# A decoder trunk's MLP: the norm's factor 1/rms² moved from the up projection to the token-major output, and the up weights regrouped

## The chip, the cores and the metric

The kernel runs on one core of one Trainium2 chip. The metric is the device time of one execution in microseconds, the median of several runs; beside it there is one profiled execution, whose trace the text reads. The engines are TensorE (PE: matmuls; PEld: its weight loads), VectorE (DVE), ScalarE (ACT), GpSimd (POOL) and SyncE (SP, which issues most of the DMAs).

## What is computed

A trunk of two layers over 512 tokens of width 1024, all in float32. Layer 0 mixes tokens with a gated DeltaNet, layer 1 with a convolution module; each layer then has a cross-attention into a memory of 256 tokens, and an MLP. The change is in the MLP:

```
def rms_norm(x, g):
    return x * rsqrt(mean(x * x, axis=-1) + 1e-6) * g

def sq_relu_mlp(h, w_up, w_down):        # w_up (1024, 4096), w_down (4096, 1024)
    return square(relu(h @ w_up)) @ w_down

h = h + sq_relu_mlp(rms_norm(h, mlp_norm[layer]), w_up[layer], w_down[layer])
```

After the second layer a final rms_norm is applied. The factor 1/rms is one positive number per token. So relu commutes with it, the square makes it 1/rms², and it may be multiplied in before the relu, or once per token behind the down projection.

## The kernel before

**Precision.** A float32 product is made of three matmuls in a rounded format: each operand is split into a high part (a cast, on ScalarE) and a low part (the operand minus its high part, on VectorE), and `mm3` (line 290) issues high x high, low x high and high x low into one PSUM bank. TensorE's 7298 matmuls are mostly of this kind.

**Weights.** All weights come through one list of units of 128 x 1024 values (`order`, `loads`, `need`; lines 150 to 220). `wload` (line 227) issues a unit's DMA from SP into a `raw` buffer, of which there are six; units of the down projection that are sums of weight blocks get DMAs with accumulation from GpSimd's queue (`more`, line 237). `wsplit` (line 241) casts a unit into `wh` on ScalarE (line 251) and subtracts on VectorE into `wl` (line 255, recorded under the helper's line 71). `wnext` (line 264) hands out the next unit and first issues the loads and splits of units ahead: three `wh`/`wl` pairs exist (`NW`), so the split of a unit can start when the unit three before it has been used.

**The MLP** (`mlp7`, line 1078) goes over the 4096 hidden columns in four groups of 1024 (`g`). In each group there is first the up projection, then the down projection.

- Up: hidden columns are rows of the result, tokens its columns. Eight tiles of 128 x 512 are made, each from one weight unit of 1024 rows by 128 columns with 24 matmuls of 512 columns (`proj`). `up_ev` (line 1096) takes a bank out: VectorE does max(., 0) x `rb` (`rl`), ScalarE squares it (`u`). `rb` holds 1/rms of every token, spread over all partitions. It is made in `Norm.stat` (line 401): two matmuls with a matrix of ones (`ssq`), a Sqrt on ScalarE, a reciprocal on VectorE (`rb`, line 408). They are issued inside the second up unit of group 0, and the first bank is taken out only after that (the list `first`). Tiles come in pairs (hidden blocks 0 and 4, 1 and 5, ...); `early` (line 1106) prepares the first of a pair for the down projection and `late` (line 1110) both: sums, differences and splits of 256-column halves.
- Down: the product is made by a scheme that needs seven block products for eight (`dn7`, line 1121). Tokens are rows. Each product takes two weight units and fills two banks, which `evict` and `into` (lines 1151 and 1160) add into accumulators `acc` on VectorE, or copy there on ScalarE if the accumulator is new. In the last group an order of its own applies (`LAST7`), in which the product T2 is followed by six accumulations from SBUF to SBUF.
- Residual: in layer 0 the accumulators are transposed back at the end (`outs`). In layer 1 the residual is transposed into the accumulators during group 0 (`turn`, line 1088), and after the last group `final` (line 1208) applies the last norm: squares with a sum on ScalarE, a Sqrt, a reciprocal on VectorE, two scalings, and the output DMA.
- In layer 0, group 3, `mid` calls `mem_gain` (line 885) between up and down: 16 operations on the memory for the next layer, half on ScalarE and half on VectorE.

**Order.** The program is written as one sequence. The framework makes the semaphores and gives each engine one fixed sequence, close to the order of the text; an engine doesn't overtake in its own sequence at run time. Buffers of 128 x 512 come from one pool of 69 (`slot`).

Of the kernel before, what the change touches and what calls it, by code (L numbers as in the profile page):

```python
# [10 lines left out]
AF = mybir.ActivationFunctionType  # L11
# [26 lines left out]
def tile_trunk(ctx, tc, xT, memT, x_d, mem_d, prm_d, adt_d, bdw_d, tap_d, fin_d, w_ab, w_kq, w_v, w_z, w_dno, w_pw1, w_pw2,  # L38
# [144 lines left out]

    def plan_mlp7(layer):
        for g in range(4):
            for i in range(4):
                plan(("up", layer, g * 4 + i), w_up[layer, g * 4 + i])
# [53 lines left out]
    def wsplit():  # L241
# [5 lines left out]
        raw = combos7(i, j[0], hf) if kind == "dn7" else ws["raw"].pop(need[u])  # L247
# [13 lines left out]
        if kind == "dn7":  # L261
            after7(i, j[0], hf)

    def wnext(key, hf):
        i = ws["next"]
        assert order[i] == (key, hf), (order[i], key, hf)
        while ws["load"] <= need[min(i + NRAW + 1 + 2 * (order[i][0][0] in ("up", "dn7")), len(order) - 1)]:
            wload()
# [3 lines left out]
        return ws["hl"].pop(i)  # L272

# [94 lines left out]
    class Norm:  # L368
        def __init__(self, gname):
            self.g, self.acc, self.xs, self.n, self.side = gname, None, [], 0, None  # L370
# [12 lines left out]
        def square(self, h, e=pool, side=False):  # L383
# [12 lines left out]
            if self.n == KT:  # L396
                if self.side:
                    tt(dve, self.acc, self.acc, self.side, ALU.add)
                self.hl = split(self.acc, "sq")
# [678 lines left out]
    def mlp7(layer, norm, hres, nxt=None, mid=None):  # L1078
# [9 lines left out]
        def turn(i):  # L1088
# [4 lines left out]
            act.copy(a, ps)  # L1093
            acc[n, m, c] = a

        def up_ev(ps):
            t = slot(s="rl")
            stt(t, ps, 0.0, norm.rb, ALU.max, ALU.mult)
            u = slot(s="u2")
            act.activation(u, t, AF.Square)  # L1100
            return u
# [19 lines left out]
        def dn7(g, ops):  # L1121
# [29 lines left out]
            def into(key, c, ps, op=ALU.add):  # L1151
                k = key + (c,)
                if k not in acc:
                    acc[k] = acc_tile(key)
                    act.activation(acc[k], ps, AF.Copy, scale=1.0 if op == ALU.add else -1.0)
                else:
# [531 lines left out]
    n2 = Norm("mlp_norm0")  # L1688
# [5 lines left out]
    n5 = Norm("mlp_norm1")  # L1694
# [13 lines left out]
ACC_CV = (("p",), (1, 0), (0, 0))  # L1708
ORDER7 = [("11", "11", "a", True), ("R3", "T3", "b", True), ("S1", "T1", "c", True), ("12", "21", "a", False),
# [78 lines left out]
def _layout(np, i):  # L1788
# [36 lines left out]
    halves = [8 * g + m for g in range(4) for m in (0, 4, 1, 5, 2, 6, 3, 7)]  # L1825
    r["w_up"] = np.stack([_pack_a(np, i["mlp_w_up"][j], halves) for j in range(2)])
# [19 lines left out]
```

## Time and profile before

| | |
|---|---|
| median of 3 runs | 1466.11 us (1464.77 to 1466.46) |
| the profiled execution's own time | 1465.14 us |
| its span in the trace | 1463.4 us |
| granted TensorE clock, mean | 0.998 |
| busy: TensorE, VectorE, ScalarE, GpSimd | 99%, 73%, 53%, 18% |
| MLP of layer 0, first up matmul | at 473.4 us |
| MLP of layer 1, last up stage ends, last operation | about 1418 us, 1459 us |

The trace gives each instruction's start and duration, and for a wait what ended it. Lines are line numbers of the kernel; where a helper records an operation the line is the helper's (71 for `tt`, 77 for `stt`), so one goes by the tile's name: `wl<-raw,wh` is an operation that reads `raw` and `wh` and writes `wl`. A TensorE matmul's duration contains its way through the array; the distance between two starts is its pace.

### The profile page before, as it was taken

Reading aid. Unit: us, or ns where it says so; the run is one execution under the profiler, and the core shown is the slowest. Engines: PE = TensorE matmul, PEld = TensorE weight load, DVE = VectorE, ACT = ScalarE, POOL = GpSimd, SP = SyncE. Lnnn points to the kernel's source line nnn. Section 1 sums busy time; section 2 is a strip of 40 time slices with the busy share of each in tenths; the row PEclk is TensorE's granted clock in tenths of the full one; section 3 lists DMA queues with packets and bytes.
Section 4 is the critical chain, followed back from the end, with each engine's and each line's share of the span. In section 5 each row is a group of like instructions: output and inputs, shape, how many; then the busy total and the mean of one; then the engine's idle time right before and its main releaser. Section 6 shows DMA issues by size and latency. Waiting matters only on the chain.

```text
span 1463.4 us, 19623 instructions
## 1 busy us (share of the span) xinstructions
PE 1452.9 (99%) x7298; PEld 1225.5 (84%) x7298; DVE 1065.2 (73%) x1615; ACT 771.2 (53%) x1326; POOL 266.8 (18%) x289
## 2 busy tenths in 40 slices
PE   9999999999999999999999999999999999999997
PEld 7888889988888888888888889988888888888886
DVE  6879889867646766767679899985555776767677
ACT  7766865655434464435355655564444544434354
POOL 1411310103113000010000486402113010000100
PEclk9999999999999999999999999999999999999999
DMA  8232124442213666584766624533214566575853
GB/s 283 84 115 73 59 87 158 132 143 87 72 44 108 166 165 179 140 199 136 202 159 215 185 82 162 179 129 100 72 51 127 139 169 177 135 210 131 229 144 87
DMA packets 62735, 201.82 MB, mean 138 GB/s; under 512 B 7728, under 2 KB 10032, under 8 KB 62640
## 3 DMA queue, kind: packets, MB, share of 16 engines
q1 hardware_dynamic: 52416, 164.39, 33.4%
q0 software_dynamic: 9792, 35.66, 14.3%
q8 instruction: 57, 0.93, 0.3%
q10 hardware_dynamic: 432, 0.52, 0.1%
q14 instruction: 38, 0.31, 0.1%
HBM read 197.66 MB, written 2.10 MB: 136 GB/s over the span
## 4 chain that ended last, share of the span: by engine, by line
PE 94%; DVE 3%; ACT 2%; DMA 1%; issue 0%; POOL 0%; SPq 0%; POOLq 0%; DVEq 0%
PE up L292 8%; PE up L294 8%; PE up L293 8%; PE dn L1130 6%; PE dn L1128 6%; PE dn L1129 6%; PE pw L294 3%; PE pw L292 3%; PE pw L293 3%; PE h L292 3%; PE h L293 3%; PE h L294 3%; PE xo L293 2%; PE xo L294 2%; PE q L292 2%; PE q L293 2%
## 5 line engine op out<-in xcount | busy, mean ns | idle before, releaser
L251 ACT CAST wh<-raw 128x1024 fp32r<-128x1024 f32 x259 | 271.6, 1051 | 358.7 <-issue 97.0
L71 DVE TENSOR_TENSOR wl<-raw,wh 128x1024 fp32r<-128x1024 f32 (+1 forms) x250 | 304.2, 1219 | 104.3 <-ACT wh L251 98.5
L292 PE MATMUL up<-xh,wh 128*128 128x512 f32 x512 | 199.7, 390 | 0.0
L294 PE MATMUL up<-xh,wl 128*128 128x512 f32 x512 | 199.3, 389 | 0.0
L293 PE MATMUL up<-xl,wh 128*128 128x512 f32 x512 | 199.2, 389 | 0.0
L294 PEld LDWEIGHTS up<-xh,wl 128*128 128x128 f32 x512 | 96.1, 188 | 20.1
L293 PEld LDWEIGHTS up<-xl,wh 128*128 128x128 f32 x512 | 96.2, 188 | 19.8
L292 PEld LDWEIGHTS up<-xh,wh 128*128 128x128 f32 x512 | 96.1, 188 | 19.7
L239 POOL DMA_DIRECT2D t<-w_dn x48 | 42.1, 915 | 354.2 <-DVE wl L71 239.0
L1128 PE MATMUL dn<-wh,ah 128*128 128x512 f32 x256 | 99.8, 390 | 0.0
L1130 PE MATMUL dn<-wl,ah 128*128 128x512 f32 x256 | 99.6, 389 | 0.0
L1129 PE MATMUL dn<-wh,al 128*128 128x512 f32 x256 | 99.6, 389 | 0.0
L77 DVE SCALAR_TENSOR_TENSOR rl<-up,rb 128x512 f32<-128x512 f32 x64 | 44.1, 690 | 58.4 <-PE up L294 58.4
L1358 DVE SCALAR_TENSOR_TENSOR ca<-x,prm,ca 128x512 f32<-128x512 f32 x112 | 82.3, 752 | 3.9 <-ACT ca L1355 1.5
L251 ACT CAST wh<-t 128x1024 fp32r<-128x1024 f32 x44 | 46.4, 1055 | 55.8 <-PE dn L1129 43.7
L71 DVE TENSOR_TENSOR wl<-t,wh 128x1024 fp32r<-128x1024 f32 x44 | 53.7, 1223 | 29.5 <-ACT wh L251 29.3
L292 PE MATMUL h<-xh,wh 128*128 128x512 f32 x184 | 73.7, 400 | 0.0
L71 POOL TENSOR_TENSOR sq<-sq,sq 128x512 f32<-128x512 f32 x28 | 45.4, 1621 | 148.3 <-ACT sq L385 134.2
L294 PE MATMUL h<-xh,wl 128*128 128x512 f32 x184 | 71.9, 391 | 0.0
L293 PE MATMUL h<-xl,wh 128*128 128x512 f32 x184 | 71.7, 390 | 0.0
L71 DVE TENSOR_TENSOR acc<-acc,dn 128x512 f32<-128x512 f32 x100 | 67.3, 682 | 1.2
L71 DVE TENSOR_TENSOR al<-u,ah 128x512 fp32r<-128x512 f32 x64 | 44.1, 688 | 21.4 <-ACT ah L331 21.4
(385 smaller groups left out, 3560.1 us busy)
## 6 DMA issues: line engine op xcount, KB each, us to landing
raw<-w_dn SPq DMA_DIRECT2D x68, 512.0 KB, 3.7
raw<-w_up SPq DMA_DIRECT2D x64, 512.0 KB, 4.3
t<-w_dn POOLq DMA_DIRECT2D x48, 512.0 KB, 6.0
raw<-w_pw SPq DMA_DIRECT2D x24, 512.0 KB, 3.7
raw<-w_dn POOLq DMA_DIRECT2D x20, 512.0 KB, 5.9
raw<-w_k SPq DMA_DIRECT2D x16, 512.0 KB, 3.6
raw<-w_vv SPq DMA_DIRECT2D x16, 512.0 KB, 4.1
t<-w_dn SPq DMA_DIRECT2D x16, 512.0 KB, 3.5
```

Source lines behind the costliest of these rows:

```text
L71: r = e.tensor_tensor(out=o, in0=a, in1=b, op=op)
L77: return dve.scalar_tensor_tensor(out=o, in0=a, scalar=s, in1=b, op0=op0, op1=op1)
L239: nc.gpsimd.dma_start(out=t, in_=a, accum_op=ALU.add)
L251: ins = [act.copy(h, raw)]
L292: pe.matmul(ps, wh, xh, start=first, stop=False)
L293: pe.matmul(ps, wh, xl, start=False, stop=False)
L294: pe.matmul(ps, wl, xh, start=False, stop=last)
L1128: pe.matmul(ps, xh, w[0][:, s], start=opens and k == 0, stop=False, skip_group_check=True)
L1129: pe.matmul(ps, xl, w[0][:, s], start=False, stop=False, skip_group_check=True)
L1130: pe.matmul(ps, xh, w[1][:, s], start=False, stop=k == 3, skip_group_check=True)
L1358: first["tap"] = dve.scalar_tensor_tensor(out=a, in0=src, scalar=w, in1=a, op0=ALU.mult, op1=ALU.add)
```

## The change

The statistic isn't spread over partitions any more. `columns` makes it as four columns of a 128 x 4 tile, one number per token with tokens on partitions: `ms` = mean square + eps, `r2` = 1/ms, `r2n` = -1/ms. The up projection's result is taken out without a factor, by two ScalarE operations, Relu and Square. The factor is applied in the last group: the accumulators so far are scaled by `r2`, and what is added to them takes `r2` or `r2n` on the way. In layer 1 the residual is multiplied by `ms` when it is put into the accumulators, so that the later scaling gives it back.

A weight unit of the up projection now has 512 rows by 256 columns. `plain` makes two tiles from two such units: unit 0 feeds both banks with the first half of the sum, unit 1 both with the second half. A group is two half groups `sg` of four units each.

The diff also brings a path `fast` for the up projection with seven products (with `UP7`, `block_up`, `combos_up`), which is entered for `g >= PLAIN`; PLAIN is 4 and g runs from 0 to 3. `x_sums`, which makes that path's operands, is called from `side` in group 0 at the units 4 to 7. `fast` and its plans are left out here.

```
     class Norm:
...
+        def columns(self):
+            ps = psum("ssq")
+            for c in range(4):
+                pe.matmul(ps[:, c:c + 1], self.acc[:, c * P:(c + 1) * P], ones[:, 0:1], start=True, stop=True)
+            self.ms, self.r2, self.r2n = [keepc(4, s + str(self.cols)) for s in ("ms", "r2", "r2n")]
+            ts(dve, self.ms, ps[:, 0:4], 1.0 / 1024, ALU.mult, EPS, ALU.add)
+            dve.reciprocal(self.r2, self.ms)
+            ts(dve, self.r2n, self.r2, -1.0, ALU.mult)
...
                 if self.side:
                     tt(dve, self.acc, self.acc, self.side, ALU.add)
-                self.hl = split(self.acc, "sq")
+                if self.cols is None:
+                    self.hl = split(self.acc, "sq")
...
         def turn(i):
...
-            act.copy(a, ps)
+            act.activation(a, ps, AF.Copy, scale=norm.ms[:, 2 * n + c:2 * n + c + 1])
...
-        def up_ev(ps):
-            t = slot(s="rl")
-            stt(t, ps, 0.0, norm.rb, ALU.max, ALU.mult)
-            u = slot(s="u2")
-            act.activation(u, t, AF.Square)
-            return u
+        def relu2(x, o):
+            act.activation(o, x, AF.Relu)
+            act.activation(o, o, AF.Square)
+            return o
...
             def into(key, c, ps, op=ALU.add):
...
+                elif g == 3 and key != ("p",):
+                    col = slice(2 * key[0] + c, 2 * key[0] + c + 1)
+                    dve.scalar_tensor_tensor(out=acc[k], in0=ps, scalar=(norm.r2 if op == ALU.add else norm.r2n)[:, col],
+                                             in1=acc[k], op0=ALU.mult, op1=ALU.add)
                 else:
                     tt(dve, acc[k], acc[k], ps, op)
...
+        def x_sums(k):
+            a, b = slot(s="xa"), slot(s="xb")
+            ga, gb = pc(norm.g, k), pc(norm.g, 4 + k)
+            tt(dve, b[:, 0:256], hres[k][:, 256:512], hres[k][:, 0:256], ALU.subtract)
+            act.activation(b[:, 0:256], b[:, 0:256], AF.Copy, scale=ga)
+            stt(a[:, 0:256], hres[4 + k][:, 256:512], gb, b[:, 0:256], ALU.mult, ALU.subtract)
+            stt(a[:, 256:512], hres[k][:, 0:256], ga, a[:, 0:256], ALU.mult, ALU.subtract)
+            stt(b[:, 256:512], hres[4 + k][:, 0:256], gb, a[:, 0:256], ALU.mult, ALU.subtract)
+            for t, names in ((a, ("R2", "S1")), (b, ("R3", "S4"))):
+                for name, p in zip(names, pair(split(t, "x"))):
+                    X[name].append(p)
+
+        def plain(g, sg, side):
+            us = []
+            for b in range(2):
+                pss = [psum("up") for _ in range(2)]
+                for a in range(2):
+                    w = wnext(("up", layer, g * 4 + sg * 2 + b), a)
+                    for j in range(2):
+                        for k in range(4):
+                            c = slice(k * 256 + j * P, k * 256 + j * P + P)
+                            mm3(pss[j], (w[0][:, c], w[1][:, c]), xs[4 * a + k], a == k == 0, a == 1 and k == 3)
+                            if (g, sg, b, a, j, k) == (0, 0, 0, 1, 0, 1):
+                                norm.columns()
+                    side(4 * sg + 2 * b + a)
+                us.append([relu2(ps, slot(s="u2")) for ps in pss])
+                for j in range(2):
+                    if b:
+                        late(ops[2 * sg + j], us[0][j], us[1][j])
+                    else:
+                        early(ops[2 * sg + j], us[0][j])
...
+        def side(i):
+            if layer == 1:
+                if i:
+                    turn(i - 1)
+                if i == 7:
+                    turn(7)
+            if i > 3:
+                x_sums(i - 4)
...
         for g in range(4):
-            ops, us = [{} for _ in range(4)], []
-            for i in range(8):
-                w = wnext(("up", layer, g * 4 + i // 2), i % 2)
-                ps = psum("up")
-                proj(w, xs, ps, inside={1: norm.stat} if (g, i) == (0, 1) else None)
-                first.append(ps)
-                if (g, i) == (0, 0):
-                    continue
-                while first:
-                    us.append(up_ev(first.pop(0)))
-                    if len(us) % 2:
-                        early(ops[len(us) // 2], us[-1])
-                    else:
-                        late(ops[len(us) // 2 - 1], us[-2], us[-1])
-                if (layer, g) == (1, 0) and i > 1:
-                    turn(i - 2)
-            if (layer, g) == (1, 0):
-                turn(6)
-                turn(7)
+            ops = [{} for _ in range(4)]
+            if g == 3:
+                for n, m, c in [k for k in acc if len(k) == 3]:
+                    act.activation(acc[n, m, c], acc[n, m, c], AF.Copy, scale=norm.r2[:, 2 * n + c:2 * n + c + 1])
+            for sg in range(2):
+                if g < PLAIN:
+                    plain(g, sg, side if g == 0 else lambda i: None)
+                else:
+                    fast(g, sg)
...
-    n2 = Norm("mlp_norm0")
+    n2 = Norm("mlp_norm0", 0)
...
-    n5 = Norm("mlp_norm1")
+    n5 = Norm("mlp_norm1", 1)
...
+PLAIN = 4
...
-    halves = [8 * g + m for g in range(4) for m in (0, 4, 1, 5, 2, 6, 3, 7)]
-    r["w_up"] = np.stack([_pack_a(np, i["mlp_w_up"][j], halves) for j in range(2)])
+    r["w_up"] = f(np.stack(i["mlp_w_up"][:2]).reshape(2, 2, 4, 128, 4, 2, 2, 256).transpose(0, 4, 6, 5, 3, 1, 2, 7)
+                  .reshape(2, 16, 128, 2048))
```

More of the change, by code (lines that the diff above doesn't have):

```diff
@@ L182, in block, with block_up @@
         return w_dn[layer, g * 4 + BLOCKS7.index(b)][:, h * 1024:(h + 1) * 1024]
+    def block_up(layer, g, sg, b):
+        a = int(b[0]) - 1
+        return w_up[layer, g * 4 + sg * 2 + int(b[1]) - 1][:, a * 1024:(a + 1) * 1024]
     def plan_mlp7(layer):
         for g in range(4):
-            for i in range(4):
-                plan(("up", layer, g * 4 + i), w_up[layer, g * 4 + i])
+            if g < PLAIN:
+                for i in range(4):
+                    plan(("up", layer, g * 4 + i), w_up[layer, g * 4 + i])
+            else:
+                for sg in range(2):
+                    n = len(loads)
+                    for b in UPLOAD:
+                        loads.append([block_up(layer, g, sg, b)])
+                    for u in range(7):
+                        order.append((("ups", layer, g, sg), u))
+                        need.append(n + (UPLOAD.index(UP7[u][1]) if u < 3 else 3))
             n, base7[layer, g] = len(loads), len(order)
@@ L262, in wsplit @@
             after7(i, j[0], hf)
+        if kind == "ups" and hf == 2:
+            t = TU
+            t["12"] = ws["raw"].pop(need[u] - 1)
+            for x, y in (("22", "12"), ("12", "11"), ("11", "22"), ("21", "11")):
+                tt(pool, t[x], t[x], t[y], ALU.add)
     def wnext(key, hf):
@@ L272, in wnext, with combos_up @@
         return ws["hl"].pop(i)
+    TU = {}
+    def combos_up(u, hf):
+        name = UP7[hf][1]
+        if hf < 3:
+            TU[name] = ws["raw"].pop(need[u])
+            return TU[name]
+        return TU[{"T1": "12", "T2": "11", "T4": "21", "T3": "22"}[name]]
     T7 = {}
```

64 lines of the change are left out of this document (60 added, 4 removed).

## The prediction

> **What bounds the kernel now.** I read the head of the page first, then what TensorE waited for, then single stretches.
>
> ```profile
> span 1463.4 us, 19623 instructions
> ...
> PE 1452.9 (99%) x7298; PEld 1225.5 (84%) x7298; DVE 1065.2 (73%) x1615; ACT 771.2 (53%) x1326; POOL 266.8 (18%) x289
> ...
> PE 94%; DVE 3%; ACT 2%; DMA 1%; issue 0%; POOL 0%; SPq 0%; POOLq 0%; DVEq 0%
> ```
>
> ```profile
> PE warm L130 <- POOL ones L127: 1.2, 1, 1.2
> PE h L1558 <- ACT xh L378: 1.0, 1, 1.0
> PE pw L294 <- POOL wl L71: 0.2, 1, 0.2
> PE dn L1130 <- DVE wl L71: 0.2, 1, 0.2
> ```
>
> TensorE is busy for 1452.9 of 1463.4 us, and 94% of the chain that ended last is its own matmuls. In the second fence (waits of TensorE: total, times, longest) two waits belong to the first microseconds; the other two are 0.2 us each. So there is nothing between the stages to win back: the time is the number of matmuls times their pace, plus the two ends. The pace is read from the first matmul of a stretch of the up projection and from the first of the down projection behind it, 78 matmuls later:
>
> ```profile
> 499.75 0.39 PE L292 MATMUL up<-xh,wh 128*128 128x512 f32 x1
> ...
> 517.43 0.39 PE L1128 MATMUL dn<-wh,ah 128*128 128x512 f32 x1
> ```
>
> 17.68 us / 78 = 0.2267 us for one matmul of 512 columns. One weight unit of the up projection feeds 24 of them, 5.44 us; one of the down projection feeds 12, 2.72 us.
>
> The other engines have room, but not everywhere. The next rows are windows of layer 0: nearly the whole up projection of group 0, and the down projection of group 3 (PE, PEld, DVE, ACT, POOL busy).
>
> ```profile
> 473.40:516.90 43.50, 43.50 (x193) 36.01 (x192) 31.92 (x45) 22.57 (x32) 3.36 (x4) 1.00 0.62 154
> 762.20:800.30 38.10, 37.94 (x175) 31.29 (x174) 35.20 (x51) 20.46 (x28) 2.32 (x6) 1.00 0.69 214
> ```
>
> VectorE is busy for 31.92 of 43.5 us in the first and for 35.20 of 38.1 us in the second. That second place is also where one of the 0.2 us waits lies.
>
> **Matmuls.** The projection itself issues as many as before: a group was 8 units x 8 tiles x 3 = 192, and is now 2 x 2 x 2 x 2 x 4 x 3 = 192. The path with seven products isn't entered, because g runs to 3 and PLAIN is 4. What goes on TensorE is the statistic, two matmuls per layer; what comes is four matmuls of one column each.
>
> ```profile
> 480.22 0.40 PE L404 MATMUL ssq<-sqh,ones_r 128*128 128x512 f32 x1
> 480.46 0.39 PE L404 MATMUL ssq<-sql,ones_r 128*128 128x512 f32 x1
> 480.69 0.39 PE L292 MATMUL up<-xh,wh 128*128 128x512 f32 x1
> ```
>
> The two old ones take 480.69 - 480.22 = 0.47 us. The new ones read plain fp32 tiles, and the trace has such calls at full clock, three in a row for small sums (the first, and the matmul behind the last), and in the warm-up:
>
> ```profile
> 44.91 0.30 PE L530 MATMUL gsum<-g,ones 128*128 128x32 f32 x2
> ...
> 45.56 0.94 PE L536 MATMUL dt<-R,L 128*128 128x512 f32 x3
> ```
>
> ```profile
> L130 PE MATMUL warm<-ones 128*128 128x128 f32 x18 | 4.0, 418 | 1.2 <-POOL ones L127 1.2
> ```
>
> Nine warm-up calls are 18 instructions, so a plain fp32 call is two matmuls with two weight loads. Three calls of 32 columns take 45.56 - 44.91 = 0.65 us, 0.22 each. A call with one column isn't in the trace. It can't cost less than nothing, nor, being smaller, clearly more than 0.22; I take 0.22, the nearest row. Four cost 0.87, the old pair 0.47: +0.4 us per layer, **+0.8 us** (-0.9 to +0.8).
>
> **VectorE and ScalarE in the steady state.** Mean durations:
>
> ```profile
> L71 DVE TENSOR_TENSOR wl<-raw,wh 128x1024 fp32r<-128x1024 f32 x246 | 302.5, 1232 | 99.6 <-ACT wh L251 98.5
> ...
> L77 DVE SCALAR_TENSOR_TENSOR rl<-up,rb 128x512 f32<-128x512 f32 x64 | 44.1, 690 | 58.4 <-PE up L294 58.4
> L71 DVE TENSOR_TENSOR al<-u,ah 128x512 fp32r<-128x512 f32 x64 | 44.1, 688 | 21.4 <-ACT ah L331 21.4
> ...
> L71 DVE TENSOR_TENSOR s<-u,s 128x256 f32<-128x256 f32 x64 | 27.0, 421 | 1.1
> ...
> L408 DVE RECIPROCAL rb<-sd 128x512 f32<-128x512 f32 x5 | 16.8, 3353 | 2.9 <-ACT sd L406 2.9
> ...
> L71 DVE TENSOR_TENSOR acc<-acc,acc 128x512 f32<-128x512 f32 x12 | 7.4, 683 | 0.0
> ...
> L77 DVE SCALAR_TENSOR_TENSOR y<-acc,sm,gt 128x512 f32<-128x512 f32 x4 | 2.9, 749 | 0.1
> ```
>
> ```profile
> L251 ACT CAST wh<-raw 128x1024 fp32r<-128x1024 f32 x259 | 271.6, 1051 | 358.7 <-issue 97.0 <-PE dn L1129 82.4 <-PE up L293 77.8
> ...
> L1100 ACT ACTIVATE u<-rl 128x512 f32<-128x512 f32 x64 | 40.1, 626 | 10.4 <-DVE rl L77 10.2
> ...
> L378 ACT ACTIVATE xh<-h,prm 128x512 fp32r<-128x512 f32 x40 | 28.7, 722 | 17.4 <-DVE h L71 17.4
> ...
> L1155 ACT ACTIVATE acc<-dn 128x512 f32<-128x512 f32 x12 | 7.2, 598 | 2.1 <-PE dn L1130 2.1
> ```
>
> VectorE loses 64 of `rl` (44.1 us), two `rb` reciprocals (6.7) and two 128x512 splits. ScalarE gains 64 Relu from PSUM (nearest row L1155, 598 ns: 38 us) and 16 scalings of 128x512 with a pointer scale (L378, 722 ns: 12 us). I cost all of this at nothing, because TensorE covers it: the cast and subtraction of a weight unit (1.05 + 1.23 us) may run two units ahead, within 5.44 us even in the down projection. The three small VectorE operations of the new statistic and the two reciprocals gone aren't waited for by TensorE either; the trace shows no TensorE wait at the old statistic. Without that cover the Relus would cost up to 38 us. The weight DMAs keep count and size, and SP's and POOL's queues their order.
>
> **What isn't spread evenly** is left, in four places.
>
> 1. The operand sums for the unused path. `x_sums` runs four times in group 0 of each layer; its results are read only in `fast`, but the warm-up bank is read by nobody either and its matmuls stand in the trace, so I expect these to be issued. One needs four 128x256 operations and two of 128x512 on VectorE, 4 x 0.42 + 2 x 0.69 = 3.1 us. In the last four units (21.8 us) VectorE then has 4 subtractions of weights 4.9, two `early` (0.42 + 0.69) 2.2, two `late` (4 x 0.42 + 2 x 0.69) 6.1 and 12.3 of sums: 25.5 us, 3.7 too many. ScalarE in layer 1 has 4 casts 4.2, four Relu and four Square 4.9, splits about 4.5, sums 4 x 1.65, turns 4 x 0.72: 23 of 21.8. Neighbours overlap by a little (two `y` of ScalarE take 1.34 us together in the tail's rows below, not 2 x 0.72), so 1 to 4 us spill into the down projection. There the third unit has 5.44 - 1.05 - 1.23 = 3.2 us of slack. I take 0.5 us of stall per layer, **+1.0** (0 to 7.4, the whole excess twice).
>
> 2. Both `late` of a half group now come behind the same matmul pair. Before, one of them came 10.9 us earlier. At a plain boundary one more `late`, 3.1 us less the `rl` of 0.7, stands ahead of the next subtractions; the 3.2 us of slack just hold it: 0. Not so in layer 0, group 3, where `mem_gain` follows. The chain there, in time order (start, us):
>
> ```profile
> 770.31 2.84 DVE ml L77 x7
> 773.15 1.15 DVE wl L71
> 774.34 0.50 PE dn L1130
> ```
>
> Seven `ml` operations ran ahead of the `wl` that TensorE needed, and the matmul took 0.50 instead of 0.23. What VectorE has left behind the last up matmul there grows by about 0.7 us: part of the first `late` is done before it. I take **+0.5** (-0.3, the stall gone, to +2.4).
>
> 3. In group 3 six accumulations from SBUF become scalar_tensor_tensor: 749 ns (`y`) against 683 (`acc<-acc,acc`), 0.4 us per layer ahead of two `wl`. I take **+0.2** in all (0 to 0.8).
>
> 4. The activation table. Sqrt needs a load where Exp came last, and the old statistic did it early in each MLP:
>
> ```profile
> 479.95 1.28 ACT L406 ACT_TABLE_LOAD   x1
> 481.24 0.69 ACT L406 ACTIVATE sd<-ssq,eps_rms 128x512 f32<-128x512 f32 x1
> ```
>
> With Sqrt gone from there, the load moves to the next Sqrt. Behind layer 0 that is the Sqrt of the convolution's norm:
>
> ```profile
> 819.17 0.69 ACT L406 ACTIVATE sd<-ssq,eps_rms 128x512 f32<-128x512 f32 x1 [1.31 <-PE ssq L404]
> ```
>
> ScalarE sat idle for 1.31 us before it, waiting for TensorE; the load's 1.28 us fit: 0. Behind layer 1 it is the Sqrt of the final norm, in the tail:
>
> ```profile
> 1451.27 0.63 ACT L1215 ACTIVATE fq<-acc 128x512 f32<-128x512 f32 x1 [2.51 <-DVE acc L71]
> ...
> 1452.51 0.47 ACT L1221 ACTIVATE sm<-sm,sm 128x1 f32<-128x1 f32 x2
> 1453.21 1.34 ACT L1231 ACTIVATE y<-y,sm 128x512 f32<-128x512 f32 x2 [0.23 <-DVE sm L1226]
> ...
> 1457.10 0.63 ACT L1215 ACTIVATE fq<-acc 128x512 f32<-128x512 f32 x1 [0.66 <-DVE acc L71]
> ```
>
> ```profile
> 1455.72 0.75 DVE L77 SCALAR_TENSOR_TENSOR y<-acc,sm,gt 128x512 f32<-128x512 f32 x1
> 1456.39 0.68 DVE L71 TENSOR_TENSOR acc<-acc,dn 128x512 f32<-128x512 f32 x1
> ```
>
> There the load stands ahead of 1452.51, and `y`, the next reciprocal and the next `y` on VectorE (1455.72) go 1.28 us later. The last accumulation (1456.39) is queued behind that `y` on VectorE, and the last Square (1457.10) behind both. Were the accumulation first, ScalarE's own order still costs about 0.6 us: its last `y` would end at 1457.7. I take **+1.0** (0.6 to 1.28; 0 if the load is put elsewhere). The Trainium skill (ScalarE: Activation LUTs, What ACT_TABLE_LOAD costs) gives about 1283 ns for a load and 1380 ns more for a drain. By it the tail would lose up to 2.66. The trace agrees with the load, but the Sqrt at 481.24 starts 0.01 us after it, so it shows no drain behind.
>
> **Sum.** 0.8 + 1.0 + 0.5 + 0.2 + 1.0 = 3.5 us on the profiled execution's 1465.14 (span 1463.4 and 1.7 around it): 1468.6. That execution lies 1.0 under the median of the runs, 1466.11, so the median becomes **1469.6 us**, +0.24%. A measurement of this kernel can tell about 0.2%, 2.9 us, from no change, so this sits near the line.
>
> **Rivals.**
> - *All covers hold.* The sums and the paired `late` disappear in idle time, the load lands in a gap of ScalarE (the 2.51 us idle before 1451.27, if it were issued earlier). Then 0.8 is left, at most 1.5: 1466.9. For it: TensorE hasn't one wait over 0.2 us in either MLP. It decides if the excess in place 1 stays below the 3.2 us of slack and the load isn't next to its Sqrt; the trace speaks against the second, where each load stands right before its user.
> - *VectorE becomes the bound at the ends of the up stages.* If sums and `late` go ahead of `wl` in VectorE's order, as `ml` did, the excess of 3.7 us comes twice whole, and the six other boundaries lose some 0.5 each: 7.4 + 3 + the 1.8 of matmuls and tail = 12, less what overlaps: about 1475. It needs the backlog at a boundary to exceed 3.2 us. Against: a list of ready work rarely runs in the worst order.
> - *The relief of VectorE wins.* 44 us less there, and the two waits of 0.2 us go: at most -0.5, 1465.6, as nothing else waits.
> - *The change isn't what it says.* Seven products for eight would take 24 matmuls, 5.4 us, from each group; only a group past PLAIN would have it, and there is none.
>
> **Chances.** Forecast, +1.5 to +6: 0.55, of which 0.35 above +2.9 and 0.20 below. Covers hold: 0.20. VectorE bound: 0.20, all slower. Relief: 0.02, within 0.2%. Not what it says, or anything else on the fast side that I don't see: 0.03, of which 0.02 over 0.2%. Slower 0.35 + 0.20 = 0.55; same 0.20 + 0.20 + 0.02 + 0.01 = 0.43; faster 0.02. The range leaves out the last two (0.05), a quarter of the second case (0.05) and the upper half of the third (0.10): 1466.3 to 1475.
>
> **What would show it.** Four fp32 calls in 0.8 to 0.9 us where two matmuls stood; `x_sums` on VectorE in group 0, and at the third to fifth weight unit behind it a TensorE wait for `wl`; the wait near 774 grown to about 0.8; a table load ahead of the first Sqrt of the tail, and last output 1 us later behind the last matmul. The forecast is wrong if TensorE waits for operands (`sh`, `al`) or a weight DMA rather than `wl`, or if its matmul pace in the up stage is no longer 0.2267.

## The result

The changed kernel takes 1477.8 us (median of three runs, 1476.06 to 1479.84) against 1466.11: a ratio of 1.0083, 95% interval 1.006 to 1.0106. It is slower by 11.7 us. The forecast of 1469.6 had the sign, and its range, up to 1475, missed the time. The profiled execution of the changed kernel took 1479.84 us.

The head of its page, and what TensorE waited for (total, times, longest):

```profile
span 1478.1 us, 19757 instructions
...
PE 1459.3 (99%) x7310; PEld 1227.7 (83%) x7310; DVE 1037.7 (70%) x1601; ACT 825.4 (56%) x1426; POOL 266.8 (18%) x289
...
PE 93%; DVE 3%; ACT 2%; issue 1%; DMA 1%; POOL 0%; SPq 0%; DVEq 0%; POOLq 0%; ACTq 0%
```

```profile
PE pw L326 <- POOL wl L71: 2.9, 1, 2.9
PE h L1683 <- ACT xh L410: 1.4, 1, 1.4
PE warm L130 <- POOL ones L127: 1.2, 1, 1.2
PE dn L1168 <- ACT sh L363: 1.2, 1, 1.2
PE dn L1170 <- DVE wl L71: 1.2, 1, 1.2
PE pw L325 <- DVE xl L77: 0.6, 1, 0.6
PE dn L1168 <- ACT acc L1195: 0.5, 1, 0.5
```

VectorE was relieved, from 1065.2 to 1037.7 us, and the whole got longer: TensorE now waits where it didn't. Two of the seven waits belong to the first microseconds (`h`, `warm`). Of the other five, three are in the MLP (`dn`). The longest and the one for `xl` are in `pw`, the pointwise product of the convolution module, which the change doesn't touch.

The windows that answer to the two of before (nearly the whole up projection of layer 0's group 0; the down projection of its group 3):

```profile
475.40:518.90 43.50, 43.50 (x197) 36.11 (x197) 26.68 (x44) 23.75 (x37) 3.39 (x4) 1.00 0.60 149
...
767.30:805.40 38.10, 36.91 (x170) 30.11 (x169) 35.56 (x52) 21.47 (x30) 2.31 (x6) 1.00 0.62 202
```

In the first VectorE (third pair) is 5.2 us less busy and TensorE has no gap; in the second VectorE has no less to do than before, and TensorE 1.2 us of idle time.

To see what each wait costs I cut the span at the first matmul of each stage. The lengths in this table are distances between two such starts in the two traces; "T4" is the first matmul of the last product of layer 0's MLP, behind which come the handover to the convolution, the convolution and the cross-attention.

| stage | before | after | difference |
|---|---|---|---|
| start to layer 0's first up matmul (same code) | 473.42 | 475.45 | +2.03 |
| layer 0, group 0, up | 44.01 | 44.47 | +0.46 |
| layer 0, group 0, down | 38.08 | 40.67 | +2.59 |
| groups 1 and 2, group 3 up, both layers | 43.52, 38.08 | 43.52, 38.08 | 0 each |
| layer 0, group 3, down up to T4 | 34.80 | 36.13 | +1.33 |
| T4 to layer 1's first up matmul | 328.14 | 333.41 | +5.27 |
| layer 1, group 0, up / down | 47.65 / 38.19 | 48.24 / 38.47 | +0.59 / +0.28 |
| layer 1, group 3, down | 37.88 | 38.25 | +0.37 |
| last matmul's start to the end | 7.83 | 9.59 | +1.76 |

The first row is the same code. It lay between 472.7 and 473.4 in the three profiled kernels with the MLP of before and between 473.4 and 475.5 in the others; with one trace of each, chance and a small cost can't be told apart, and the 2.03 isn't counted as a cost of the change here. The profiled execution lies 2.04 over its median. The fifth row is the forecast's place 2; the sixth, the stretch behind T4 (the expectations call it the stretch from outs), it didn't have at all. That stretch in both kernels, in order of time (start, duration, engine, line): T4, the statistic `ssq` of the convolution's norm, its reciprocal `rb`, the first gate `xp`, GpSimd's weight subtractions, the matmul that waits for them, and layer 1's up projection. Before:

```profile
797.03 0.48 PE L1128 MATMUL dn<-wh,ah 128*128 128x512 f32 x1
817.91 0.50 PE L404 MATMUL ssq<-sqh,ones_r 128*128 128x512 f32 x1
819.90 3.35 DVE L408 RECIPROCAL rb<-sd 128x512 f32<-128x512 f32 x1 [0.18 <-ACT sd L406]
825.72 0.75 DVE L77 SCALAR_TENSOR_TENSOR xp<-pa,prm,sg 128x512 f32<-128x512 f32 x1 [0.20 <-ACT sg L1296]
852.54 4.76 POOL L71 TENSOR_TENSOR wl<-raw,wh 128x1024 fp32r<-128x1024 f32 x2
854.99 0.50 PE L294 MATMUL pw<-xh,wl 128*128 128x512 f32 x1 [0.23 <-POOL wl L71]
1125.17 0.39 PE L292 MATMUL up<-xh,wh 128*128 128x512 f32 x1
```

After:

```profile
803.45 0.48 PE L1168 MATMUL dn<-wh,ah 128*128 128x512 f32 x1
827.40 0.50 PE L446 MATMUL ssq<-sqh,ones_r 128*128 128x512 f32 x1
829.38 3.35 DVE L450 RECIPROCAL rb<-sd 128x512 f32<-128x512 f32 x1 [0.18 <-ACT sd L448]
837.50 0.75 DVE L77 SCALAR_TENSOR_TENSOR xp<-pa,prm,sg 128x512 f32<-128x512 f32 x1 [0.81 <-ACT sg L1421]
862.67 4.69 POOL L71 TENSOR_TENSOR wl<-raw,wh 128x1024 fp32r<-128x1024 f32 x2
865.07 0.63 PE L326 MATMUL pw<-xh,wl 128*128 128x512 f32 x1 [2.85 <-POOL wl L71]
1136.86 0.39 PE L324 MATMUL up<-xh,wh 128*128 128x512 f32 x1
```

Counted from T4, `rb` comes 22.9 us later before and 25.9 after, `xp` 28.7 and 34.1, GpSimd's `wl` 55.5 and 59.2. GpSimd is the last link: it adds up the tap products that ScalarE makes from `xp`, its two subtractions of weights come behind them, and a TensorE matmul needs these. Before, that chain already made TensorE wait 0.23 us: at its end it had no slack. After, `xp` comes 5.4 us later. A part of that is taken up on the way, where GpSimd waits for ScalarE's products (5.25 us before, 4.32 after); its `wl` comes 3.7 us later, and TensorE waits 2.85.

What is different there is the order on the engines, which is fixed when the program is built. On VectorE, from the first residual addition, before: h h xl h xl h wl xl acc acc xl wl. After: h h wl xl h wl xl h acc acc xl wl xl. A weight unit is prepared two additions earlier, ahead of the operands `xl` of the convolution. TensorE's own order follows: 59 matmuls of `pw` stand ahead of `ssq` before and 68 after, and it waits 0.6 us for an `xl` on the way. 9 x 0.2267 + 0.6 = 2.6 us is most of the 3.0 that `rb` loses. A second exchange of the same kind (a cast and a `wl` ahead of the first sigmoid and of `xp`) stands behind the rest of `xp`'s 5.4.

### The profile page after: what moved, and what is told of

The parts are those of the page before. It is cut to its first block, busy times and chain, and to the rows that moved or that the text cites. A ratio compares the mean times of both kernels' runs of the same rounds, so it can differ in the third digit from the quotient of the medians.

```text
span 1478.1 us, 19757 instructions
## 1 busy us (share of the span) xinstructions
PE 1459.3 (99%) x7310; PEld 1227.7 (83%) x7310; DVE 1037.7 (70%) x1601; ACT 825.4 (56%) x1426; POOL 266.8 (18%) x289
## 4 chain that ended last, share of the span: by engine, by line
PE 93%; DVE 3%; ACT 2%; issue 1%; DMA 1%; POOL 0%; SPq 0%; DVEq 0%; POOLq 0%; ACTq 0%
PE up L324 8%; PE up L326 8%; PE up L325 8%; PE dn L1168 6%; PE dn L1170 6%; PE dn L1169 6%; PE pw L326 3%; PE pw L325 3%; PE pw L324 3%; PE h L324 3%; PE h L325 3%; PE h L326 3%; PE xo L325 2%; PE q L325 2%; PE q L324 2%; PE q L326 2%
## 5 line engine op out<-in xcount | busy, mean ns | idle before, releaser
L1139 ACT ACTIVATE u<-up 128x512 f32<-128x512 f32 x64 | 37.4, 593 | 41.5 <-PE up L326 41.5
L1170 PEld LDWEIGHTS dn<-wl,ah 128*128 128x128 f32 x256 | 48.0, 188 | 12.4 <-DVE wl L71 2.4
L1168 PEld LDWEIGHTS dn<-wh,ah 128*128 128x128 f32 x256 | 48.1, 188 | 10.1 <-ACT ah L363 0.2
```

The lines of the kernel that those rows point to most:

```text
L1139: act.activation(o, x, AF.Relu)
L1168: pe.matmul(ps, xh, w[0][:, s], start=opens and k == 0, stop=False, skip_group_check=True)
L1170: pe.matmul(ps, xh, w[1][:, s], start=False, stop=k == 3, skip_group_check=True)
```

## The experiments

All ran against the kernel before on the same chip (medians there 1466.1 to 1466.3). The stages are those of the table above.

| kernel | median us | ratio, 95% interval | layer 0 group 0 down | group 3 down to T4 | T4 to layer 1 up | end |
|---|---|---|---|---|---|---|
| e1_no_sums | 1475.93 | 1.0063 (1.005 to 1.0075) | 38.08 | 36.17 | 331.78 | 9.56 |
| e2_factor_only | 1474.23 | 1.0053 (1.004 to 1.0065) | 38.08 | 34.87 | 333.46 | 9.33 |
| e3_units_only | 1471.26 | 1.0036 (1.0023 to 1.0048) | 38.08 | 35.58 | 331.76 | 8.08 |
| e4_table_early | 1477.66 | 1.0082 (1.0068 to 1.0096) | 40.67 | 36.14 | 331.76 | 8.38 |
| e5_hold_handover | 1471.1 | 1.0035 (1.0022 to 1.0049) | 38.08 | 36.17 | 328.39 | 9.43 |
| e6_hold_both | 1469.93 | 1.0027 (1.0016 to 1.0038) | 38.08 | 36.12 | 327.93 | 9.59 |
| e7_gain_early | 1474.41 | 1.0054 (1.0042 to 1.0067) | 38.08 | 34.38 | 333.53 | 9.57 |
| e8_plain1 | 1545.8 | 1.0544 (1.0529 to 1.0558) | - | - | - | - |
| e9_all_held | 1467.0 | 1.0006 (0.9997 to 1.0014) | 38.08 | 34.38 | 327.92 | 8.35 |
| e10_before_forced | 1469.52 | 1.003 (1.0019 to 1.0042) | 38.08 | 34.84 | 331.87 | 7.85 |
| e11_sums_spread | 1466.95 | 1.0007 (0.9998 to 1.0016) | 38.08 | 34.38 | 327.92 | 8.35 |
| e12_before_gain_early | 1465.49 | 0.9998 (0.9989 to 1.0007) | 38.08 | 34.34 | 328.16 | 7.83 |

### The parts of the change, one by one

**Without the sums.** The changed kernel less the calls whose results nobody reads:

```
-            if i > 3:
-                x_sums(i - 4)
```

> The changed kernel without the calls of x_sums, whose results nothing reads. By the traces of before and after, the down stage of group 0 is 2.6 us longer in layer 0 and 0.3 in layer 1. Theory S (the sums fill VectorE and ScalarE at that boundary): these 2.9 us go, the rest of the loss stays, about 1474.9. Rival R (what fills the engines there is the pair of late operations behind one matmul pair): the two stages stay within 0.5 us of after, 1477.5.

Group 0's down projections fall from 40.67 to 38.08 and from 38.47 to 38.18: the sums cost 2.9 us, as theory S has it. The two stalls that go in layer 0 are these of the changed kernel, which wait for an operand and for a bank, not for a weight:

```profile
540.50 0.73 PE L1168 MATMUL dn<-wh,sh 128*128 128x512 f32 x2 [1.20 <-ACT sh L363]
...
544.16 0.50 PE L1168 MATMUL dn<-wh,sh 128*128 128x512 f32 x1 [0.55 <-ACT acc L1195]
```

The way to the first of them begins with the order on ScalarE. The sums' casts stand there ahead of the last two Relu of the up stage. These start 11.8 us into the down projection, and 0.9 us into it without the sums (the stage begins at 519.93 and 518.57); `s` on VectorE and `sh` follow them. In the changed kernel, then without the sums:

```profile
531.74 1.08 ACT L1139 ACTIVATE u<-up 128x512 f32<-128x512 f32 x2
```

```profile
519.50 0.59 ACT L1139 ACTIVATE u<-up 128x512 f32<-128x512 f32 x1
```

In layer 1 the Relu come as late (11.9 us), yet only 0.3 us is lost; why was not followed up. The stretch behind T4 stays 3.6 us too long, so the sums aren't its cause.

**The factor alone, the units alone.** The first is the kernel before with `columns`, `relu2` and the scaled accumulations and its old weight units; the second the changed kernel with 512 x 256 units and the old statistic and `up_ev`. Both are without the sums.

```
-            t = slot(s="rl")
-            stt(t, ps, 0.0, norm.rb, ALU.max, ALU.mult)
...
-            act.activation(u, t, AF.Square)
+            act.activation(u, ps, AF.Relu)
+            act.activation(u, u, AF.Square)
```

> The kernel before with the factor moved alone: Relu and Square on ScalarE, columns, the scaled accumulations of group 3; up units of 1024 rows by 128 columns as before, no x_sums. Theory F (the scaled accumulations fill VectorE in the last down stage of layer 0, the handover to the convolution comes late, and GpSimd's weight split there with it; the tail loses a table load): 0.8 of matmuls, 1.3 in that stage, 5.3 in the convolution, 1.5 in the tail, about 1475. Rival U (the regrouped units, with both late operations at the end, make the backlog): 0.8 and 1.5 alone, about 1468.4.

> The changed kernel with the regrouped up units alone: 1/rms spread over partitions and multiplied in before the square as before, unscaled accumulations, no x_sums. Theory F: no more than 0.5 us, about 1466.6, and no wait for the weight split on GpSimd in the convolution beyond that of before (0.4 us). Rival U: the last down stage of layer 0 and the convolution lose their 6.6 us here, about 1473.

Neither theory holds alone: the loss behind T4 comes with either part, 5.3 us with the factor (1.7 of them the clock, see the end) and 3.6 with the units. In both builds a weight unit has moved ahead of an `xl`, and the first gate has the changed order. In group 3's down projection the factor costs 0.07 us alone, the units 0.78, both together 1.33.

**The table load early.** At the end of layer 1's up stage of group 0 the Sqrt table is asked for ahead of time:

```
+            if (layer, i) == (1, 7):
+                root_table()
```

> The changed kernel with one Sqrt of a constant on ScalarE at the end of layer 1's first up stage, so that the table is there before the tail. Theory T (the load in the tail costs its duration): the stretch from the last matmul's start to the end, 9.6 us after and 7.8 before, becomes 8.3 or less, total 1.3 us below after, 1476.5. Rival (the tail is longer because of the order on VectorE): less than 0.4 us of it goes, 1477.4.

The end falls from 9.59 to 8.38, close to theory T's 8.3. ScalarE in the tail of the changed kernel:

```profile
1465.03 0.63 ACT L1259 ACTIVATE fq<-acc 128x512 f32<-128x512 f32 x1 [2.63 <-DVE acc L1198]
...
1465.78 1.28 ACT L1265 ACT_TABLE_LOAD   x1
1467.07 0.29 ACT L1265 ACTIVATE sm<-sm,sm 128x1 f32<-128x1 f32 x1
```

and with the early load:

```profile
1463.44 0.64 ACT L1259 ACTIVATE fq<-acc 128x512 f32<-128x512 f32 x1 [2.62 <-DVE acc L1198]
...
1464.20 0.29 ACT L1265 ACTIVATE sm<-sm,sm 128x1 f32<-128x1 f32 x1
```

The first `sm` comes 2.04 us behind the start of `fq` with the load there and 0.76 without. Of the end's 1.76 us, 1.2 are the load; the other 0.55 were not followed up. The kernel as a whole doesn't gain theory T's 1.3: its median is 1477.66 against 1477.8. At its new place the load stands on ScalarE among the late casts of the sums; TensorE waits there 0.81 us for the cast of a weight unit (at 1197.31), and layer 1's down projection of group 0 grows from 38.47 to 39.33. With the early load and without the sums it takes 38.17 (e9 below).

### The order at the handover

**Holding it.** `hold` places the next weight unit's cast in the build behind the second cast of the convolution's operands, and its subtraction behind the fourth residual addition; nothing is added to the program's work.

```
+        behind_act, behind_dve = ws.pop("hold", (None, None))
...
+        with tc.issue_after(behind_dve.ins) if behind_dve else nullcontext():
+            ins.append(tt(pool if gp else dve, lo, raw, h.bitcast(F32), ALU.subtract))
...
+                if i == 3:
+                    ws["hold"] = second, made
```

> The changed kernel without the sums, and with the first weight unit that is prepared behind layer 0's outs held back: its cast on ScalarE behind the second operand cast of the convolution's input, its subtraction on VectorE behind the fourth residual addition, so that the handover to the convolution has the order of the kernel before. The next unit is still prepared ahead of the first gate (sigmoid and the product xp). Theory O (the order is the cause, at the handover itself): the stretch from outs to layer 1's first up matmul falls from 331.8 (the kernel without sums) to 328.1 to 329.0, the kernel to about 1472.5. Rival O2 (the order at the first gate decides, which is not restored here): the wait in front of the handover goes but that at the end of the pointwise products stays, 330.5 to 331.8. Rival L (not the order but the lateness of what layer 0 leaves on ScalarE and VectorE): 331.5 or more, with the waits only moved.

The second kernel also holds the next unit behind the first gate (`ws["hold"] = sig, stt(...)` in `pw_ev`).

> The same, and the second unit held too: cast behind the first sigmoid, subtraction behind the first product xp, so that the first gate goes ahead of the weights as in the kernel before. Theory O and rival O2 both give 328.1 to 329.0 in the stretch from outs to layer 1's first up matmul; rival L 331.5 or more. If O2 is right, this one gains 2 to 3 us over the one that holds the first unit alone; if O is right, under 0.7.

Theory O: 331.78 falls to 328.39 with the handover alone, 327.93 with both, against 328.14 before. L falls. O2 isn't decided: with the first unit held, the first gate has the order of the kernel before again without a hold of its own (on VectorE behind `rb`: wl sg pa xp wl in both; in the changed kernel wl sg pa wl xp, where `sg` and `pa` are the gate's inputs). So the two exchanges go together, and which of them costs how much stays open. The matmul that waited 2.86 us waits, with the handover held, as long as in the kernel before:

```profile
800.18 0.48 PE L1170 MATMUL dn<-wh,ah 128*128 128x512 f32 x1
...
858.40 0.50 PE L328 MATMUL pw<-xh,wl 128*128 128x512 f32 x1 [0.24 <-POOL wl L71]
...
1128.57 0.39 PE L326 MATMUL up<-xh,wh 128*128 128x512 f32 x1
```

**Forcing it on the kernel before.** That takes nothing from the change but the order: the next weight unit is prepared at the second residual addition (`wsplit` is called there), its subtraction behind that addition, and the first operand behind the unit.

```
+                if i == 1:
+                    ws["hold"] = made
+                    wsplit()
                 if k:
-                    nxt.parts(i - 1, new[i - 1])
+                    nxt.parts(i - 1, new[i - 1], behind=ws["pair"] if i == 1 else (None, None))
```

> The kernel before, nothing of the change in it, but with the handover's order of the changed kernel forced on it: the weight unit after next is prepared between the second and the third residual addition, its cast ahead of the first operand cast and its subtraction ahead of the first xl. No instruction more or less. Theory O (the order alone makes the loss): the stretch from outs to layer 1's first up matmul rises from 328.1 to 331.0 to 333.5, with a wait of 2 to 3 us for POOL's wl near the end of the pointwise products; the kernel goes to 1469 to 1472. Rival L (the order hurts only behind the later accumulations of the changed kernel): 328.1 to 329.2.

The same loss appears in a kernel without any of the change: 331.87 us behind T4, 1469.52 in all (+3.4). Its chain:

```profile
796.95 0.48 PE L1133 MATMUL dn<-wh,ah 128*128 128x512 f32 x1
820.79 0.50 PE L409 MATMUL ssq<-sqh,ones_r 128*128 128x512 f32 x1
822.98 3.35 DVE L413 RECIPROCAL rb<-sd 128x512 f32<-128x512 f32 x1 [0.38 <-ACT sd L411]
831.06 0.75 DVE L77 SCALAR_TENSOR_TENSOR xp<-pa,prm,sg 128x512 f32<-128x512 f32 x1 [0.81 <-ACT sg L1304]
856.23 4.71 POOL L71 TENSOR_TENSOR wl<-raw,wh 128x1024 fp32r<-128x1024 f32 x2
858.63 0.50 PE L297 MATMUL pw<-xh,wl 128*128 128x512 f32 x1 [2.86 <-POOL wl L71]
```

From T4, `rb` comes after 26.0, `xp` after 34.1, GpSimd's `wl` after 59.3: the numbers of the changed kernel to a tenth. The exchange at the first gate comes here too, without being forced. So the order alone makes this loss. Why the build tips the order when the up projection's code changes was not tried and stays open.

### Group 3, the sum of the costs, the unused path

**mem_gain ahead of group 3**, in the changed kernel without the sums and in the kernel before:

```
+            if g == 3 and mid:
+                mem_gain(1, 0)
+                mem_gain(1, 1)
...
-    h, rest = mlp7(0, n2, h, n3, lambda: (mem_gain(1, 0), mem_gain(1, 1), taps(NTAP)))
+    h, rest = mlp7(0, n2, h, n3, lambda: taps(NTAP))
```

> The changed kernel without the sums, with mem_gain (the seven ml operations and their like) issued ahead of layer 0's group 3 up stage, not behind it. Theory M (the wait at the start of group 3's down projection comes from mem_gain behind both late of a half group): the stretch from there to outs falls from 36.17 to 34.3 to 34.9, as the wait of the kernel before (0.5) goes too; group 3's up stage, 43.52, grows by 0 to 0.3. Rival: the two late alone are enough; 35.5 or more. The later stretches are not touched by either, except that the order at the handover may turn out another again.

> The kernel before with mem_gain ahead of group 3's up stage: the only wait of its MLPs that a move could take away. If mem_gain is the cause there too, the stretch from group 3's down projection to outs falls from 34.80 to 34.3 to 34.4, and the kernel by 0.3 to 0.5 us, which a measurement of it can't tell from no change; a rival (the backlog of the late operations alone) leaves 34.6 to 34.8.

Theory M in both: 36.17 falls to 34.38, and 34.80 to 34.34; group 3's up stage stays at 43.52. In the changed kernel the eight `ml` run at 782.74, behind the second `late`, and the stall comes only at 797.12, when the six accumulations of T2 have come on top:

```profile
782.74 3.29 DVE L77 SCALAR_TENSOR_TENSOR ml<-mem,prm,mh 128x256 fp32r<-128x256 f32 x8
...
795.84 2.35 DVE L71 TENSOR_TENSOR wl<-raw,wh 128x1024 fp32r<-128x1024 f32 x2
```

```profile
797.12 0.50 PE L1170 MATMUL dn<-wl,ah 128*128 128x512 f32 x1 [1.17 <-DVE wl L71]
```

The kernel before can't be told from itself with the move (0.9998, 0.9989 to 1.0007).

**All four taken away:** no sums, early table, early `mem_gain`, both holds.

> The changed kernel with the four found costs taken away at once: no sums, the table load early in layer 1's MLP, mem_gain ahead of group 3's up stage, and both weight units held at the handover and the first gate. What is left by the stages measured so far: the columns (+0.46 and +0.59 in the first up stages), the scaled accumulations in the last down projection (+0.37), the tail (+0.55), less the stall that mem_gain made already in the kernel before (-0.42) and the convolution stretch at 327.9 to 328.4. Theory A (these places are the whole difference): a span of 1464.4 to 1465.8, a ratio of 1.000 to 1.0015. Rival B (a cost is left that no stage has shown, or one that moves when another goes): a ratio of 1.0025 or more.

Theory A: 1467.0 us, 1.0006 (0.9997 to 1.0014), a span of 1464.8. TensorE's waits all lie in the first 24 us:

```profile
PE warm L130 <- POOL ones L127: 1.2, 1, 1.2
PE rb L396 <- DVE rstd L458: 0.6, 1, 0.6
PE h L1693 <- ACT xh L412: 0.4, 1, 0.4
```

So the table of stages holds the whole difference. By the stages 1.3 us are left (0.46 + 0.59 + 0.37 + 0.52 at the end, less 0.42 up to T4 and 0.22 behind it), which the interval doesn't tell from nothing: with these four costs away, the factor's move and the regrouped units together neither gain nor lose an amount that can be measured.

**The sums put back**, one to every second unit of group 1's up stage:

```
-                    plain(g, sg, side if g == 0 else lambda i: None)
+                    plain(g, sg, side if g == 0 else (lambda i: x_sums(i // 2) if i % 2 == 0 else None) if g == 1 else lambda i: None)
```

> The kernel with the four costs taken away, and the sums put back, one to every second unit of group 1's up stage in place of the last four units of group 0. Theory P (place: only their crowding at the end of an up stage costs): every up stage 43.5 to 43.7, every down projection 38.1 to 38.3, the kernel within 0.5 us of the one without sums. Rival W (their work costs wherever it is): 1.5 us or more in the stages of group 1 or of group 0's down projection.

Theory P: 1466.95, no stage longer than without them. Some 23 us more of VectorE's work (1037.1 us busy against 1013.9; the prediction had 12.3 in each layer) cost nothing there and 2.9 us at the end of group 0's up stages.

**The path that the sums are for**, PLAIN at 1:

```
-PLAIN = 4
+PLAIN = 1
```

> The changed kernel with its constant PLAIN at 1 in place of 4: groups 1 to 3 of each layer compute the up projection with seven products in place of eight, the path for which the sums and the unit shape were made. It has 24 fewer matmuls of 0.2267 us in each of six groups: 5.44 us each. Theory C (TensorE's count decides; the covers of the steady state hold): 43.5 becomes 38.1 in each such up stage, the kernel falls by 25 to 33 us, to 1445 to 1453, less where a handover turns out worse. Rival V (VectorE or ScalarE cannot keep up with the additional operations between products): the stages stay above 40 and the kernel above 1460.

This kernel changes part of the computation, so it is read for its time alone: its path gathers two products in each half of one bank and opens the halves one after the other. The Trainium skill (PSUM — Partial Sum Buffer, The four PSUM rules) says that a second opening matmul in a bank clears the marks of the first, so that the next matmul there overwrites the sum; no run here tests it. Theory C falls: the kernel is 80 us slower, and the up stage of layer 0's group 1 takes 50.6 us, not 38.1 (559.85 to 615.49, less 5.0 in which matmuls of the down projection go between). Its matmuls of 256 columns mostly start 0.12 us apart; 336 of them are 40.3. Most of the rest is three waits of 1.1, 1.3 and 5.0 us; behind the longest, twenty matmuls start 0.21 us apart. Ahead of that wait GpSimd adds weight blocks, and VectorE's operations on SBUF take two to four times as long as elsewhere (0.68 us for 128 x 512, 1.23 for 128 x 1024). VectorE, then GpSimd, then TensorE:

```profile
582.34 0.68 DVE L71 TENSOR_TENSOR uP<-uP,up 128x512 f32<-128x512 f32 x1
...
585.12 2.89 DVE L71 TENSOR_TENSOR uP<-uP,u 128x512 f32<-128x512 f32 x1
...
590.68 3.36 DVE L71 TENSOR_TENSOR wl<-raw,wh 128x1024 fp32r<-128x1024 f32 x1
...
593.97 0.68 DVE L71 TENSOR_TENSOR al<-uP,ah 128x512 fp32r<-128x512 f32 x1
```

```profile
581.31 11.66 POOL L71 TENSOR_TENSOR raw<-raw,raw 128x1024 f32<-128x1024 f32 x4 [10.29 <-DVE wl L71]
```

```profile
594.10 0.58 PE L1331 MATMUL up<-xh,wl 128*128 128x256 f32 x1 [5.01 <-DVE wl L71]
```

Rival V has the sign, but its reason was the number of operations, and in this stage they are also stretched while GpSimd adds. No run leaves GpSimd's sums out, and the other stages were not followed, so how much of the 80 us is which stays open. No kernel here beats both by an amount that can be measured.

## Why the prediction was wrong

The step that failed is the list "What isn't spread evenly is left, in four places". There is a fifth, the handover from layer 0's MLP to the convolution, which the sum put at nothing without a reason, and it is the largest: 5.27 us in the profiled execution, of which 3.6 are the order and 1.6 the clock behind the stall. The profile had two signs of it that the prediction read as nothing: the 0.2 us that TensorE waited for GpSimd's `wl` in `pw`, taken as proof that nothing waits, was the end of a chain of 55 us with nothing to spare there; and the fixed order was taken as given although the text of the program around it changed. The sign of the forecast isn't luck, as the terms that it had came to 7.4 us; but these alone would have put the time inside the range, with several of them mis-sized. The other steps:

- **Matmuls, +0.8:** 0.46 and 0.59 by the stages, about 1.05, above the bound of 0.8. The four calls take 0.80 us where the old pair took 0.47 (forecast 0.87), and the matmul behind them starts 0.33 us ahead of the next (483.39) and not 0.23; what more layer 1 loses was not followed up:

```profile
482.26 0.95 PE L437 MATMUL ssq<-ones,sq 128*128 128x1 f32 x8
483.06 0.49 PE L324 MATMUL up<-xh,wh 128*128 128x512 f32 x1
```

- **Steady state, 0:** right. Every stage between is the same to 0.01 us. The reshaped unit and the two ScalarE operations cost nothing there.
- **Place 1, the sums, +1.0:** the place was right, the size 2.9, and the way another. The spill was worked out against the slack of `wl`; what came late were `sh` and an accumulator's copy, behind Relu that the sums' casts had pushed back in ScalarE's order, and for them the working had no slack at all. The prediction itself names a wait for `sh` as a sign that it is wrong. Layer 0 lost 2.59 and layer 1, with more work on ScalarE, only 0.28.
- **Places 2 and 3, +0.5 and +0.2:** 1.33 in layer 0 and 0.37 in layer 1. They were added as if apart. They are one backlog: in layer 0 the units alone make 0.78, the factor alone 0.07, both 1.33 (in layer 1 0.02, 0.06 and 0.37). The working also read the wait of before as 0.50 instead of 0.23, but the one is a duration (0.39 without a wait) and the other a pace; moving `mem_gain` in the kernel before shows its worth, 0.46 (34.80 to 34.34). And the wait isn't 12 us into the down projection, where it was (774.34, the stage beginning at 762.23), but 30 us (797.12, from 767.32), behind the six accumulations.
- **Place 4, the table, +1.0:** the load costs 1.2 (early load: 9.59 to 8.38), inside its bounds; the end as a whole 1.76. The load ahead of the convolution's Sqrt was hidden in ScalarE's wait, as forecast: there too `sd` stands right behind `ssq` (`rb` waits 0.18 us for it, before and after).
- **The rival with VectorE as the bound** gave about 1475 for a reason that didn't come: the six plain boundaries lost nothing.

Sum by the stages without the start and the clock: 0.46 + 2.59 + 1.33 + 3.64 + 0.59 + 0.28 + 0.37 + 1.76 = 11.0, against 11.7 between the medians; the terms that the forecast had are 7.4 of it where it had 3.5.

## What to carry to other kernels

A wait of 0.2 us on an otherwise full engine isn't nothing: follow it back, and if the chain behind it is long and has nothing to spare, a change upstream can be paid there. Both waits of 0.2 us in the kernel before lie on chains that lost time here. When an order is fixed at build time, compare it on each engine at the stage's borders, not only inside the stage that was changed; here the exchange of a few instructions cost more than any operation that was added. Extra work on a side engine costs by where it stands and by what stands behind it in the fixed order, not by its sum: the same sums took 2.9 us at the end of a stage and none in the next.

## What the hardware showed

**The clock behind a stall.** In eight profiled executions the wait for GpSimd's `wl` in `pw` leaves 3.2 us between two starts of matmuls, 2.8 to 2.9 of it idle. In three of them (the changed kernel, e2, e7) matmuls at about half the clock followed, in the other five (e1, e3, e4, e8, e10) not. The columns are the busy times of PE, PEld, DVE, ACT and POOL, then the granted clock, the DMAs' share and GB/s, for the 3.4 us behind the stall in the changed kernel and in e1:

```profile
865.20:868.60 3.40, 3.40 (x9) 2.62 (x10) 3.40 (x7) 2.47 (x6) 3.23 (x2) 0.51 0.54 173
```

```profile
861.20:864.60 3.40, 3.40 (x15) 2.83 (x16) 3.40 (x6) 2.34 (x6) 3.25 (x2) 1.00 0.55 167
```

A clock of 0.51 and 9 matmuls against 1.00 and 15. In the changed kernel eight matmuls start 0.43 us apart and not 0.2267, 1.6 us more, which is also the difference of the stretches (333.41 and 331.78). Runs of one kernel may differ by about so much for this reason (e7: 1471.92 to 1474.74); that isn't shown, as one execution of each kernel has a trace. The Trainium skill (TensorE: Matmul & The Clock Gate, What's actually happening) says that the clock is halved after an idle window of some 3.4 us and that the windows run freely. The traces agree in part: the slow matmuls last 3.2 to 3.4 us, and the same stall has them or hasn't, but here less than 2.9 us of idle time was enough.

**VectorE beside GpSimd.** In e8 a VectorE operation of two SBUF operands took 2.89 us (585.12) while GpSimd added 128 x 1024 blocks, one of the same size 0.68 behind these (593.97), and one that reads a PSUM bank 0.68 beside them (582.34). The Trainium skill (SBUF — State Buffer, Who interferes with whom) says that a VectorE instruction with two SBUF inputs contends with a GpSimd instruction that reads SBUF; the rows above agree. So GpSimd's sums weren't free for VectorE there.
